# Layer 1 of a two-layer diffusion backbone: the output projection finishes one token tile at a time, and the MLP's first three blocks follow in pieces of 128 tokens

## The chip, the cores and the metric

The kernel runs on one core of a Trainium2 chip. The metric is the device time of one execution, in microseconds; before, the median of three runs is 1603.42 us (1602.07 to 1603.76).

## The reference

Two layers with the same weights for 256 context and 256 latent tokens, 1024 wide. Each layer mixes tokens with three parallel branches, merges them with gates, applies one output projection `W_out`, and then runs a squared-ReLU MLP. Around both halves stand RMS norms and shift, scale and gate vectors. The last layer (layer 1) needs only the latent tokens. The part that matters here, shortened:

```python
merged = g[..., 0, :] * (ys[0] @ w_branch[0])
for j in range(1, N_BRANCHES):
    merged = merged + g[..., j, :] * (ys[j] @ w_branch[j])
y_l = merged @ w_out
...
x = x + m_l[2] * rms_norm(y_l, norm_g[l, 1])
h_l = modulate(rms_norm(x, norm_g[l, 2]), m_l[3], m_l[4])
x = x + m_l[5] * rms_norm(jnp.square(jax.nn.relu(h_l @ w_mlp_up[l])) @ w_mlp_down[l], norm_g[l, 3])
```

So the MLP of a token needs the norm of the whole row of `y_l`, that is both halves of its output projection.

## The kernel before

All 512 tokens lie in four tiles of 128: tiles 0 and 1 are context, 2 and 3 are latent. Layer 1 works on tiles 2 and 3. Activations are kept as a high and a low part (`hact`, in the tile `h`), weights too, and each product is made of three matmuls: high by high, high by low, low by high. `mm_cm` (L248 to L250) holds weights in the array and streams tokens; `mm_tm` (L260 to L262) holds 128 tokens and streams 512 weight columns.

A weight block of 4096 numbers per partition arrives as two DMAs (L217, on SP's queue) into two of five slots `raw`; ScalarE casts each into the high part (L226), VectorE subtracts for the low part (L227). Blocks go in turn to the two places of `whl`, or to a place in the arena `arr` if `dst` is given. Every free place is only reused after its last reader.

In layer 1, `branch` (L1163 to L1190) makes the merged activations, eight channel tiles one after another: the sigmoid of the gate (L1163, ScalarE), the product with the branch's projection (L1180, VectorE, reading PSUM), the sum (L1185, GpSimd), high (L1189) and low part (L1190). L1128 and L1129 write the activations of the third branch that its projection reads. PSUM banks go round by `dps`.

`tm_out` with `W_out` follows: two halves of 512 output columns, each from two blocks of 512 rows. In layer 1 `seqs` asks for half 0 of tiles 2 and 3 and then half 1, where the last half is done tile by tile. One tile and half is 24 matmuls. `finish` takes each result: the sum of squares (L654, ScalarE) and the product with the gate row (L655, VectorE). `after(tt)` then runs the chain from the projection to the MLP's input for one tile: `post` (L630, L455 on GpSimd, L634), `prenorm` (squares L567, L569, L455, scaling L574 on VectorE and L576 on ScalarE, eight transposes L582 on TensorE) and `modulate` (L599 on VectorE and L597 on ScalarE from PSUM, high part L604, low part L606). In layer 1 the tiles' modulations are held back in `late` and done together when tile 3 is through.

The MLP's up projection runs through `cm_blocks`: 16 blocks of 256 columns, each two groups (`i`) of 24 matmuls. In layer 1 all of them stream the 256 latent tokens at once. `relu2` takes each group: L1330 and L1331 on ScalarE, L1332 on GpSimd, L1333 on VectorE. `nb` is 2: the first two blocks lie in `arr`, the later ones in `whl`. `gate_rows` (L620, eight transposes) makes the gate row that the MLP's end needs.

The order of the instructions on each engine is set by a scheduler from the dependencies, from priorities (`hp`) and from a few rules of order (`behind`, `set_fence`); each engine then works its own list strictly in that order.

Of the kernel before, what the change touches and what calls it, by code (L numbers as in the profile page):

```python
# [19 lines left out]
T = 512  # L20
LAT = 256
# [90 lines left out]
class Net:  # L112
# [524 lines left out]
    def tm_out(self, w, r0, act, y, yss, seqs, add, gains=None, after=None):  # L637


        nc = self.nc  # L640
        junk = self.A.get(1)
        left = {tt: 2 for tt in y}

        def finish(tt, b, ps):
            o = y[tt][:, b * 512:b * 512 + 512]
            with self.hp():
                src = ps
                if add:
                    nc.vector.tensor_tensor(out=o, in0=src, in1=o, op=ALU.add)
                    src = o  # L650
                elif not gains:
                    nc.scalar.copy(o, src)
                if gains:
                    nc.scalar.activation(junk[:, :], src, AF.Square, scale=D ** -0.5, accum_out=yss[tt][:, b:b + 1])  # L654
                    nc.vector.tensor_tensor(out=o, in0=src, in1=gains(tt)[:, b * 512:b * 512 + 512], op=ALU.mult)  # L655
            left[tt] -= 1

        for tts, halves, whole in seqs:
            for b in halves:
                ps = {}  # L660
                order = [(kh, tt) for kh in range(2) for tt in tts]
                blks = {}
                if whole:
                    order = [(kh, tt) for tt in tts for kh in range(2)]
                    blks = {kh: self.wblock(w, r0 + kh * 512, 4, b * 512, 512) for kh in range(2)}
                for kh, tt in order:
                    if kh not in blks:
                        blks[kh] = self.wblock(w, r0 + kh * 512, 4, b * 512, 512)
                    if not kh:
                        ps[tt] = self.dps()  # L670
                    self.mm_tm(ps[tt], blks[kh], 4, 0, 512, act, tt, kt0=kh * 4, start=not kh, stop=kh == 1)
                    if kh:
                        finish(tt, b, ps[tt])
            for tt in tts:
                if gains and left[tt] == 0:
                    after(tt)
        junk.free()
# [516 lines left out]
    def cm_blocks(self, loads, q0, skew, evac, done=lambda b: None, also=None):  # L1194


        segs = [(q0, T - q0)]
        b0 = 0
        if skew and q0 == 0:
            blks = [loads[b]() for b in range(2)]  # L1200
            for t0 in (0, LAT):
                for b, blk in enumerate(blks):
                    for i in range(2):
                        ps = self.dps()[:, 0:LAT]
                        self.mm_cm(ps, blk, 8, i * 128, self.hact, t0, LAT)
                        evac(b, i, ps, t0, LAT)
                    if t0:
                        done(b)
                if also:
                    also(range(t0 // 128, t0 // 128 + 2))  # L1210
            b0 = 2
        for b in range(b0, len(loads)):
            blk = loads[b]()
            for i in range(2):
                ps = self.dps()[:, 0:T - q0]
                self.mm_cm(ps, blk, 8, i * 128, self.hact, q0, T - q0)
                evac(b, i, ps, q0, T - q0)
            done(b)
# [22 lines left out]
    def layer(self, l):  # L1241
        nc, A, I = self.nc, self.A, self.I
        last = l == DEPTH - 1
        self.nd = 3 if last else 2
        w = I["w_in"][l]
        tts = list(range(4)) if not last else [2, 3]

        ysb_b, ys_b = self.acts(4)
        for hp in range(2):
            st, hv, gn, bufs = self.hgrn_dense(l, w, hp)  # L1250
# [10 lines left out]
        for hp in range(2):  # L1261
            Q, Kt, dv, bufs = pair
# [5 lines left out]
        Q, kT, sv = self.swa_dense(l, w)  # L1268
# [17 lines left out]
        sv = self.scale_vecs(l, 1)  # L1286
        y = {tt: A.get(2) for tt in tts}
        if not last:
            seqs = [((0, 1), (0, 1), False), ((2, 3), (0, 1), False)]
        else:  # L1290
            seqs = [((2, 3), (0,), False), ((2, 3), (1,), True)]
        yss = {tt: self.yss[:, tt * 3:tt * 3 + 3] for tt in tts}

        late = []

        def after(tt):
            with self.hp():
                ops = list(self.post(tt, y[tt], yss[tt]))
                if not last:
                    self.modulate(tt, sv, self.prenorm(tt, y[tt]), y[tt])  # L1300
                    return
                late.append((tt, sv, self.prenorm(tt, y[tt]), y[tt]))
                if tt == 3:
                    res = self.modulate(*late[0], ops=ops) + self.modulate(*late[1], quick=True)
                    self.set_fence(res, 1, 2)

        if not last:
            while self.pumps:
# [1 line left out]
            self.ada_late(1, range(3))  # L1310
            self.rate = 0
        self.nd, self.np = 4, 8
        nb = 2 if last else 1
        gains = lambda tt: G[1 if tt < 2 else 0]
        self.tm_out(I["w_out"][l], 0, self.hact, y, yss, seqs, False, gains, after)
        for g in G.values():
            g.free()

        q0 = 0 if not last else LAT
        n = T - q0  # L1320
        y = {tt: A.get(2) for tt in tts}
# [28 lines left out]
        for qd in range(4):  # L1350
            ab, act, wb = {}, {}, {}

            def wu(b):
                if not last and qd in (0, 3):
                    self.rate = 2 if (qd, b) >= (0, 2) else 0
                if qd == 0 and b < nb:
                    wb[b] = self.R.get(8)
                return self.wblock(I["w_mlp_up"][l], 0, 8, qd * 1024 + b * 256, 256, dst=wb[b].ap if b in wb else None)

            def done(b):  # L1360
                if b in wb:
                    wb[b].free()

            self.cm_blocks([lambda b=b: wu(b) for b in range(4)], q0, qd == 0,
                           lambda b, i, ps, t0, nn: relu2(ab, act, b * 2 + i, ps, t0, nn), done)
            if qd == 3:
                G = {s: self.gate_rows(l, 1, s) for s in ((1, 0) if not last else (0,))}
                if not last:
                    sv = self.scale_vecs(l + 1, 0)
            if last and qd == 3:  # L1370
                seqs = [((2, 3), (0,), False), ((2, 3), (1,), True)]
            elif qd == 3:
                seqs = [((0, 1), (0, 1), False), ((2, 3), (0, 1), False)]
            else:
                seqs = [(tts, (0, 1), False)]
            self.tm_out(I["w_mlp_down"][l], qd * 1024, act, y, yss, seqs, qd > 0, gains if qd == 3 else None, after)
            for b in ab.values():
                b.free()
# [37 lines left out]
```

## Time and profile before

| | |
|---|---|
| runs | 1602.07, 1603.42, 1603.76 us |
| profiled execution, own time | 1602.47 us |
| its span, first to last instruction | 1600.7 us |
| TensorE matmul busy | 1546.6 us (97%) |
| VectorE, ScalarE, GpSimd busy | 1045.6, 777.4, 393.0 us |
| mean granted TensorE clock | 0.986 of full speed |

A busy share is an average over the whole program, so the stage that is changed, about 1370 to 1430 us, is read by itself: how long TensorE waits there, what ends the waits, and how far apart its matmuls start. In the timeline a row gives start, length, engine, line, operation, tiles and shapes; a matmul's length contains a fixed part that overlaps the next, so its price in a stream is the distance from start to start. A 128x256 matmul is one that streams 256 columns.

### The profile page before, as it was taken

What the parts mean: (1) busy time and instruction counts of PE and PEld (TensorE: products, weight loads), DVE (VectorE), ACT (ScalarE), POOL (GpSimd) and SP (SyncE); (2) the same over time, 40 slices, a digit from 0 to 9 for tenths busy, and PEclk for the clock granted to TensorE, in tenths of its full rate; (3) what the DMA queues carried; (4) which work ended last, traced back from release to release, by engine and by line L of the source; (5) the groups of instructions that cost most, each with busy time, mean ns of one, the idle gap of its engine ahead of it and who ended that gap; (6) DMA issues with size and microseconds to landing.
All of it is one profiled execution on the core that took longest, in us unless ns stands there. A gap on an engine that the chain in (4) does not pass through costs nothing.

```text
span 1600.7 us, 26956 instructions
## 1 busy us (share of the span) xinstructions
PE 1546.6 (97%) x10326; PEld 1323.4 (83%) x10326; DVE 1045.6 (65%) x1897; ACT 777.4 (49%) x1588; POOL 393.0 (25%) x419
## 2 busy tenths in 40 slices
PE   6999999999999999999999999999898999989997
PEld 4788887878777778888888888999897999889996
DVE  3655544577477568777656546786668788665665
ACT  4443433446444457533424246644445656666553
POOL 1142415050420001210102011464455250121001
PEclk9999999999999999999999999999999999999999
DMA  9823234233332336466566434432334254446562
GB/s 282 236 80 119 75 114 143 80 79 115 123 93 79 115 109 211 140 202 194 176 208 191 151 106 145 125 114 78 122 106 106 67 149 125 148 139 191 185 185 92
DMA packets 209681, 220.06 MB, mean 137 GB/s; under 512 B 24400, under 2 KB 177168, under 8 KB 209552
## 3 DMA queue, kind: packets, MB, share of 16 engines
q1 hardware_dynamic: 209552, 218.34, 45.2%
q8 instruction: 81, 1.33, 0.3%
q14 instruction: 48, 0.39, 0.1%
HBM read 217.26 MB, written 1.05 MB: 136 GB/s over the span
## 4 chain that ended last, share of the span: by engine, by line
PE 85%; DVE 5%; POOL 4%; DMA 2%; ACT 2%; issue 2%; SPq 1%; POOLq 0%; DVEq 0%; ACTq 0%
PE b L248 16%; PE b L249 16%; PE b L250 16%; PE b L260 8%; PE b L261 8%; PE b L262 8%; POOL arf L919 1%; PE b L364 1%; DVE whl L227 1%; PE b L1122 1%; PE b L1109 1%; PE b L869 1%; PE b L949 1%; PE b L950 1%; PE b L853 1%
## 5 line engine op out<-in xcount | busy, mean ns | idle before, releaser
L227 DVE TENSOR_TENSOR whl<-raw,whl 128x512 fp32r<-128x512 f32 x588 | 431.4, 753 | 243.3 <-ACT whl L226 233.7
L226 ACT CAST whl<-raw 128x512 fp32r<-128x512 f32 x588 | 356.3, 620 | 256.4 <-PE b L262 129.3
L248 PE MATMUL b<-h,whl 128*128 128x512 f32 (+1 forms) x1296 | 447.6, 347 | 1.2 <-ACT arf L964 0.6
L250 PE MATMUL b<-h,whl 128*128 128x512 f32 (+1 forms) x1296 | 444.9, 344 | 0.8 <-DVE whl L227 0.8
L249 PE MATMUL b<-h,whl 128*128 128x512 f32 (+1 forms) x1296 | 444.6, 343 | 0.4 <-POOL h L606 0.3
L248 PEld LDWEIGHTS b<-h,whl 128*128 128x128 f32 x1296 | 247.9, 192 | 33.8 <-ACT whl L226 2.9
L250 PEld LDWEIGHTS b<-h,whl 128*128 128x128 f32 x1296 | 246.8, 191 | 29.5 <-issue 1.6
L249 PEld LDWEIGHTS b<-h,whl 128*128 128x128 f32 x1296 | 246.9, 191 | 28.9 <-issue 2.4
L1332 POOL TENSOR_TENSOR arf<-arf 128x256 f32<-128x256 f32 (+1 forms) x68 | 59.8, 880 | 411.3 <-ACT arr L1331 399.5
L262 PE MATMUL b<-whl,arr 128*128 128x512 f32 x384 | 149.9, 390 | 0.0
L261 PE MATMUL b<-whl,arr 128*128 128x512 f32 x384 | 149.9, 390 | 0.0
L260 PE MATMUL b<-whl,arr 128*128 128x512 f32 x384 | 149.7, 391 | 0.0
L919 POOL TENSOR_TENSOR arf<-arf,cst 32x256 f32<-32x256 f32 x104 | 94.3, 907 | 192.3 <-ACT arf L964 70.7
L260 PE MATMUL b<-whl,h 128*128 128x256 f32 (+1 forms) x416 | 129.0, 313 | 0.0
L261 PE MATMUL b<-whl,h 128*128 128x256 f32 (+1 forms) x416 | 128.7, 311 | 0.0
L262 PE MATMUL b<-whl,h 128*128 128x256 f32 (+1 forms) x416 | 128.6, 311 | 0.0
L455 POOL TENSOR_TENSOR sm<-sm,nhalf 128x1 f32<-128x1 f32 (+2 forms) x42 | 37.0, 883 | 333.5 <-DVE sm L630 242.5
L809 POOL TENSOR_TENSOR arf<-arf 128x512 f32<-128x512 f32 x56 | 75.8, 1376 | 43.7 <-ACT arf L788 24.1
L260 PEld LDWEIGHTS b<-whl,h 128*128 128x128 f32 x416 | 80.0, 192 | 6.4 <-ACT arf L753 0.8
L260 PEld LDWEIGHTS b<-whl,arr 128*128 128x128 f32 x384 | 72.1, 188 | 15.9 <-issue 1.2
L262 PEld LDWEIGHTS b<-whl,arr 128*128 128x128 f32 x384 | 72.1, 188 | 14.9
L261 PEld LDWEIGHTS b<-whl,arr 128*128 128x128 f32 x384 | 72.1, 188 | 14.5
(224 smaller groups left out, 2434.1 us busy)
## 6 DMA issues: line engine op xcount, KB each, us to landing
raw<-in_w_in_dram SPq DMA_DIRECT2D x110, 512.0 KB, 3.9
arf<-in_w_ada_dram SPq DMA_DIRECT2D x80, 512.0 KB, 4.9
raw<-in_w_mlp_down_dram SPq DMA_DIRECT2D x72, 512.0 KB, 3.8
raw<-in_w_mlp_up_dram SPq DMA_DIRECT2D x64, 512.0 KB, 4.3
raw<-in_w_out_dram SPq DMA_DIRECT2D x24, 512.0 KB, 4.2
arf<-in_w_ada_dram SPq DMA_DIRECT2D x32, 256.0 KB, 5.6
raw<-in_w_branch_dram SPq DMA_DIRECT2D x16, 512.0 KB, 3.9
raw<-in_w_in_dram SPq DMA_DIRECT2D x32, 128.0 KB, 3.3
```

Source lines behind the costliest of these rows:

```text
L226: self.behind(ops, lambda: nc.scalar.copy(r32(h), src))
L227: self.split_op = self.behind(ops, lambda: nc.vector.tensor_tensor(out=r32(l), in0=src, in1=h, op=ALU.subtract))
L248: nc.tensor.matmul(ps, wh, xh[:, t0:t0 + n], start=start and k == 0, stop=False)
L249: nc.tensor.matmul(ps, wh, xl[:, t0:t0 + n], start=False, stop=False)
L250: nc.tensor.matmul(ps, wl, xh[:, t0:t0 + n], start=False, stop=stop and k == nk - 1)
L260: nc.tensor.matmul(ps, xh, wh, start=start and k == 0, stop=False)
L261: nc.tensor.matmul(ps, xh, wl, start=False, stop=False)
L262: nc.tensor.matmul(ps, xl, wh, start=False, stop=stop and k == nk - 1)
L455: self.nc.gpsimd.tensor_tensor(out=r, in0=ms, in1=self.nhalf[:, 0:cols], op=ALU.pow)
L809: nc.gpsimd.tensor_tensor(out=kx, in0=kx, in1=view(cur, 1, [(nb - 1, 2), (2, nb // 2), (0, h)]), op=ALU.mult)
L919: nc.gpsimd.tensor_tensor(out=b[o, 0:LAT], in0=x[i], in1=self.cst[i, C_RS:C_RS + LAT], op=ALU.mult)
L1332: nc.gpsimd.tensor_tensor(out=r[:, c], in0=r[:, c], in1=r[:, c], op=ALU.mult)
```

## The change

In layer 1 the output projection now does tile 2 completely, both halves, and then tile 3. All four blocks of `W_out` are therefore held at once: the two of half 0 in `whl`, the two of half 1 in `arr`. `after` runs the whole chain for each tile when that tile is through. In `cm_blocks` the first three blocks of layer 1's MLP take the 128 tokens of tile 2, then the 128 of tile 3; the fourth block and all later ones take 256 as before. `nb` becomes 1: only the first block lies in `arr`, the second and third in `whl`.

```diff
@@ tm_out
         for tts, halves, whole in seqs:
+            if whole == "all":
+                bufs = [self.R.get(8) for _ in range(2)]
+                blks = {(b, kh): self.wblock(w, r0 + kh * 512, 4, b * 512, 512, dst=bufs[kh].ap if b else None)
+                        for b in halves for kh in range(2)}
+                for tt in tts:
+                    for b in halves:
+                        ps = self.dps()
+                        for kh in range(2):
+                            self.mm_tm(ps, blks[b, kh], 4, 0, 512, act, tt, kt0=kh * 4, start=not kh, stop=kh == 1)
+                        finish(tt, b, ps)
+                    after(tt)
+                for b in bufs:
+                    b.free()
+                continue
@@ cm_blocks
-        segs = [(q0, T - q0)]
         b0 = 0
-        if skew and q0 == 0:
-            blks = [loads[b]() for b in range(2)]
-            for t0 in (0, LAT):
+        if skew:
+            b0, step = (2, LAT) if q0 == 0 else (3, 128)
+            blks = [loads[b]() for b in range(b0)]
+            for t0 in range(q0, T, step):
                 for b, blk in enumerate(blks):
                     for i in range(2):
-                        ps = self.dps()[:, 0:LAT]
-                        self.mm_cm(ps, blk, 8, i * 128, self.hact, t0, LAT)
-                        evac(b, i, ps, t0, LAT)
-                    if t0:
+                        ps = self.dps()[:, 0:step]
+                        self.mm_cm(ps, blk, 8, i * 128, self.hact, t0, step)
+                        evac(b, i, ps, t0, step)
+                    if t0 + step == T:
                         done(b)
...
-            b0 = 2
@@ layer
-            seqs = [((2, 3), (0,), False), ((2, 3), (1,), True)]
+            seqs = [((2, 3), (0, 1), "all")]
...
-        late = []
-
         def after(tt):
             with self.hp():
-                ops = list(self.post(tt, y[tt], yss[tt]))
-                if not last:
-                    self.modulate(tt, sv, self.prenorm(tt, y[tt]), y[tt])
-                    return
-                late.append((tt, sv, self.prenorm(tt, y[tt]), y[tt]))
-                if tt == 3:
-                    res = self.modulate(*late[0], ops=ops) + self.modulate(*late[1], quick=True)
-                    self.set_fence(res, 1, 2)
+                for _ in self.post(tt, y[tt], yss[tt]):
+                    pass
+                res = self.modulate(tt, sv, self.prenorm(tt, y[tt]), y[tt], quick=last)
+                if last and tt == 3:
+                    self.set_fence(res, 3, 2)
...
-        nb = 2 if last else 1
+        nb = 1
```

TensorE, from the last matmul of the output projection into the MLP, layer 1 (`cst` by `arf` are the transposes of the chain, `cst` by `sm` those of the gate row, `h` the activations). Before:

```order
L262 MATMUL b_86<-whl,h 128x512
L582 MATMUL b_89<-cst,arf 128x128 x4
L582 MATMUL b_90<-cst,arf 128x128 x4
L582 MATMUL b_91<-cst,arf 128x128 x4
L582 MATMUL b_88<-cst,arf 128x128 x4
L620 MATMUL b_89<-cst,sm 128x128 x4
L620 MATMUL b_90<-cst,sm 128x128 x4
L248 MATMUL b_87<-h,arr 128x256
L248 MATMUL b_84<-h,arr 128x256
L249 MATMUL b_87<-h,arr 128x256
```

After:

```order
L262 MATMUL b_86<-arr,h 128x512
L582 MATMUL b_89<-cst,arf 128x128 x4
L582 MATMUL b_90<-cst,arf 128x128 x4
L620 MATMUL b_89<-cst,sm 128x128 x4
L620 MATMUL b_90<-cst,sm 128x128 x4
L248 MATMUL b_87<-h,arr 128x128
L248 MATMUL b_84<-h,arr 128x128
L248 MATMUL b_85<-h,whl 128x128
L248 MATMUL b_86<-h,whl 128x128
L249 MATMUL b_87<-h,arr 128x128
```

Only tile 2's transposes are left between the projection and the MLP, tile 3's follow 30 matmuls into the MLP. Tile 2's transposes still stand behind all of tile 3's projection. The gate row's transposes still use the two banks that the modulation has to read first.

ScalarE, between the third branch's activations (L1128) and its gates (L1163), layer 1. In the new file these lines are 14 higher: L1142 is L1128 and L1177 is L1163. Before:

```order
L621 COPY arf<-b_87 128x512
L621 COPY arf<-b_88 128x512
L1128 CAST arr<-b_91 128x128 x2
L1163 ACT_TABLE_LOAD
L1163 ACTIVATE arf<-arf 128x256 x8
```

After:

```order
L621 COPY arf<-b_87 128x512
L621 COPY arf<-b_88 128x512
L1142 CAST arr<-b_91 128x128
L226 CAST arr<-raw 128x512 x2
L1142 CAST arr<-b_91 128x128
L1177 ACT_TABLE_LOAD
L1177 ACTIVATE arf<-arf 128x256 x8
```

Two casts of the first block of `W_out` for `arr` now stand ahead of the last L1128; before, the block that arrives in the same slot was cast later.

VectorE, the end of the chain from the scaling (L574) to the low part (L606), layer 1. Before, for both tiles:

```order
L574 TENSOR_SCALAR arf<-arf,sm 128x512 x2
L599 TENSOR_SCALAR arf<-b_89,sb,M_67 128x128 x3
L599 TENSOR_SCALAR arf<-b_90,sb,M_67 128x128 x3
L599 TENSOR_SCALAR arf<-b_91,sb,M_67 128x128 x4
L604 CAST h<-arf 128x4x128
L606 TENSOR_TENSOR h<-arf,h 128x4x128 x3
```

After, for tile 2:

```order
L574 TENSOR_SCALAR arf<-arf,sm 128x512
L227 TENSOR_TENSOR arr<-raw,arr 128x512 x2
L599 TENSOR_SCALAR arf<-b_89,sb,M_67 128x128 x4
L630 TENSOR_REDUCE sm<-yss 128x1
L655 TENSOR_TENSOR arf<-b_86,arf 128x512
L227 TENSOR_TENSOR whl<-raw,whl 128x512
L604 CAST h<-arf 128x4x128
L227 TENSOR_TENSOR whl<-raw,whl 128x512
L634 SCALAR_TENSOR_TENSOR arf<-arf,sm 128x512 x2
L606 TENSOR_TENSOR h<-arf,h 128x4x128 x2
```

ScalarE after, over the same stretch:

```order
L576 ACTIVATE arf<-arf,sm 128x512
L654 ACTIVATE arf,yss<-b_86 128x512
L226 CAST whl<-raw 128x512 x2
L597 ACTIVATE arf<-b_90,M_67,sb 128x128 x4
L604 CAST h<-arf 128x4x128
L567 ACTIVATE arf,sm<-arf 128x512 x2
```

Between tile 2's modulation (L599) and its low part (L606) VectorE now does two weight subtractions and three steps of tile 3's chain (L655 and L634 twice); ahead of tile 2's L597 ScalarE now does two weight casts.

## Rows read from the trace of the kernel before

**Rows 1.** The page: busy time by engine, share of the span, instructions.

```profile
PE 1546.6 (97%) x10326; PEld 1323.4 (83%) x10326; DVE 1045.6 (65%) x1897; ACT 777.4 (49%) x1588; POOL 393.0 (25%) x419
```

**Rows 2.** Windows: length, busy by engine with counts, PEclk (granted clock), DMA share, GB/s.

```profile
1402.30:1413.50 11.20, 5.50 (x28) 4.96 (x28) 9.66 (x24) 8.59 (x21) 3.09 (x4) 0.70 0.14 53
1404.42:1411.25 6.83, 3.84 (x18) 3.84 (x19) 5.36 (x16) 4.48 (x12) 1.71 (x4) 0.50 0.16 62
1413.51:1430.42 16.91, 16.91 (x143) 16.91 (x143) 9.99 (x19) 11.24 (x24) 3.29 (x5) 1.00 0.47 156
```

**Rows 3.** TensorE's timeline from the projection's end into the MLP.

```profile
1402.04 0.39 PE L262 MATMUL b<-whl,h 128*128 128x512 f32 x1
1407.41 3.68 PE L582 MATMUL b<-cst,arf 128*128 128x128 f32 x16 [4.98 <-DVE arf L574]
1412.50 0.50 PE L248 MATMUL b<-h,arr 128*128 128x256 f32 x2 [0.40 <-DVE h L604]
1413.32 0.36 PE L249 MATMUL b<-h,arr 128*128 128x256 f32 x1 [0.32 <-DVE h L606]
```

**Rows 4.** TensorE's timeline around one L1087, the only form streaming 128 split columns.

```profile
1318.26 0.22 PE L1087 MATMUL b<-half 128*128 128x128 f32 x1
1318.32 0.33 PE L248 MATMUL b<-arr,whl 128*128 128x256 f32 x1
1318.49 0.28 PE L249 MATMUL b<-arr,whl 128*128 128x256 f32 x1
```

**Rows 5.** The weight loads (PEld) of the same stretch.

```profile
1318.27 0.19 PEld L248 LDWEIGHTS b<-arr,whl 128*128 128x128 f32 x1
1318.37 0.19 PEld L249 LDWEIGHTS b<-arr,whl 128*128 128x128 f32 x1
```

**Rows 6.** ScalarE's and TensorE's timelines before the projection.

```profile
1370.20 0.27 ACT L1128 CAST arr<-b 128x128 fp32r<-128x128 f32 x1 [0.36 <-DVE arr L1129]
1370.48 1.28 ACT L1163 ACT_TABLE_LOAD   x1
1371.77 2.57 ACT L1163 ACTIVATE arf<-arf 128x256 f32<-128x256 f32 x8
...
1373.19 0.39 PE L248 MATMUL b<-arr,whl 128*128 128x256 f32 x1
```

**Rows 7.** SP's timeline: the issue into the slot concerned; DMA issues: KB, us to landing.

```profile
1367.17 0.37 SPq L217 DMA_DIRECT2D raw<-in_w_out_dram  x1
...
raw<-in_w_mlp_up_dram SPq DMA_DIRECT2D x64, 512.0 KB, 4.3
raw<-in_w_out_dram SPq DMA_DIRECT2D x24, 512.0 KB, 4.2
```

**Rows 8.** VectorE's and ScalarE's timelines: the chain's pieces.

```profile
1372.71 1.09 DVE L1180 TENSOR_TENSOR arf<-b,arf 128x256 f32<-128x256 f32 x3 [1.92 <-PE b L250]
1395.39 0.68 DVE L655 TENSOR_TENSOR arf<-b,arf 128x512 f32<-128x512 f32 x1
1404.55 1.42 DVE L634 SCALAR_TENSOR_TENSOR arf<-arf,sm 128x512 f32<-128x512 f32 x2
1408.57 3.28 DVE L599 TENSOR_SCALAR arf<-b,sb,M 128x128 f32<-128x128 f32 x10 [0.29 <-PE b L582]
1411.88 0.56 DVE L604 CAST h<-arf 128x512 fp32r<-128x512 f32 x1
1412.48 2.04 DVE L606 TENSOR_TENSOR h<-arf,h 128x512 fp32r<-128x512 f32 x3
1410.73 1.55 ACT L597 ACTIVATE arf<-b,M,sb 128x128 f32<-128x128 f32 x4
1415.79 2.18 ACT L226 CAST whl<-raw 128x512 fp32r<-128x512 f32 x4
1424.86 0.38 ACT L1330 ACTIVATE arf<-b 128x256 f32<-128x256 f32 x1 [1.81 <-PE b L250]
1425.27 0.42 ACT L1331 ACTIVATE arr<-arf 128x256 fp32r<-128x256 f32 x1
```

## Prediction

> **What bounds the kernel now.** I read the page first: TensorE has a matmul in flight for 97% of the span, the next engine for 65% [rows 1]. So nearly everything that TensorE does is on the path, and the change can win only what TensorE waits in its stage, and loses whatever it adds to TensorE's list.
>
> Next TensorE's timeline around the hand-over from projection to MLP. The projection's last matmul starts at 1402.04; then nothing until the transposes at 1407.41, which waited for VectorE's scaling, and the MLP streams steadily only from 1413.32, when the low part (L606) is there [rows 3]. That is 11.3 us, in which TensorE does 24 transposes and two matmuls. This is all there is to win: TensorE is busy for 5.5 us of the 11.2 us window by its in-flight time, and part of the stretch runs at half the clock: 0.50 of full speed from 1404.42 to 1411.25, after the engine had stood idle since about 1402.4 [rows 2]. From 1413.51 on the clock is 1.00 and there are no gaps: the 16.91 us to 1430.42 hold 143 matmul records, two of which began earlier, so 256-column matmuls start 16.91/141 = 0.12 us apart [rows 2]. At 1430.42 the fourth block begins. From 1402.04 to there it is **28.4 us now**; the change rewrites exactly this piece.
>
> **The price of a 128-column matmul.** Three blocks are two groups of 24 matmuls each, 144 in all, of 256 columns. They become 288 of 128 columns: the same columns, twice the matmuls, and every matmul brings its own weight load (as many loads as matmuls, [rows 1]). So the question is whether a load of 128 columns hides behind a matmul of 128. The trace has one place with split operands and 128 columns, L1087. Read from start to start it costs 0.06 us (1318.26 to 1318.32), half of 0.12, which would be ideal. But the matmul behind it then needs 0.17 us to the next one (1318.32 to 1318.49) where 0.12 is usual [rows 4]: 0.05 us come back one place later, so L1087 costs 0.11. The weight loads say why: the load behind L1087 starts as L1087 starts (1318.27), the next one 0.10 us later [rows 5]. A 128-column matmul is over before the next weights are in. In a run of such matmuls each waits for a load, and I take 0.108 us for each, between the 0.10 and the 0.11. Bounds: 0.06, if loads hide after all, and 0.12, what a 256-column matmul takes. I take neither end because the two readings of rows 4 and 5 agree.
>
> The Trainium skill differs: "TensorE: Matmul & The Clock Gate", section "Back-to-back issue gap", gives about 81 ns for each matmul of 128 columns in a sustained stream of load and matmul pairs. By that figure the sum below would be +4.5 us instead of +12.2; no run of this case shows such a stream yet, and the rows above are nearer to this kernel.
>
> **The change part by part.**
>
> *The projection's order.* Same 96 matmuls, same blocks; only when they are cast changes. The first block for `arr` arrives in a slot that SP refills from 1367.17, landing 4.2 us later, at 1371.4 [rows 7]. Its two casts now stand ahead of ScalarE's last L1128, which ran at 1370.20 [rows 6]. Each cast is 2.18/4 = 0.545 us [rows 8], so ScalarE is through at 1372.5, with L1128 at 1372.7, the table load of 1.28 us at 1374.0, the first gate of about 0.4 at 1374.4, and VectorE's product L1180 of 0.4 [rows 6, 8] at 1374.9. The matmul at 1373.19 [rows 6] needs the bank that this frees, and starts at 1374.9: **+1.7 us**, with nothing behind it to hide in, since TensorE has no slack until the end of the projection. Bounds: 0, if the block lands before 1370, to 2.5, if the whole delay of L1128 counts. Two MLP loads move ahead of the last three `W_out` loads on SP's queue; each waits for a slot that comes free before the one behind it, so I price that at nothing; cover is the same slots' own wait.
>
> *The hand-over.* E' is the start of the projection's last matmul after the change (1402.04 + 1.7). Tile 2's projection ends 39 matmuls earlier, so squares, row factor and scaling of tile 2 are done by E' and its eight transposes follow at once. What is late next is the rest of its chain, because the lists now mix it with other work:
> - VectorE: L599 four times, 0.33 each [rows 8], from E'+0.95 to 2.25; tile 3's L655, 0.68, to 2.9; then a subtraction of weights that needs a cast by ScalarE.
> - ScalarE: that cast needs the second half of MLP block 2. Its slot is given up by the `arr` subtractions at about E'-1.5 (estimate: the casts follow tile 2's squares), plus 4.3 us to land [rows 7] = E'+2.8. Two casts to 3.9, four L597 (1.55) to 5.45 [rows 8].
> - VectorE again: subtraction to 4.05, L604 (0.56) to 4.6, second subtraction to 5.3, tile 3's two L634 (1.42) to 6.7, and only then tile 2's low part L606 (0.68) to about 7.3 [rows 8].
>
> The gate row's transposes wait for L597 too, and stay hidden before 7.3. So TensorE streams from **E'+7.3** (now: 11.3 after E). Four high-part matmuls slip in before. Bounds: 3.5, if nothing stands between (2.25 + 0.56 + 0.68), and 8.
>
> *The MLP's blocks.* 284 matmuls at 0.108 are 30.7 us. Tile 3's eight transposes lie among them, 0.9 us; its chain has the 26 matmuls ahead of them and the 114 behind them to hide in. Together **E'+38.9** for the start of the fourth block.
>
> *Evacuation.* Twice as many, half as wide. ScalarE needs 0.38 + 0.42 us for a 256-column group [rows 8] against 24 x 0.108 = 2.6 us of matmuls: priced at nothing; if the matmuls went at 0.06 it would still fit (1.4 us).
>
> *The clock.* The wait remains, so the clock may fall again. In the window of 6.83 us at 0.50 [rows 2] matmuls could take double: 0 to +3.4 us. I take 0: now, too, the clock was back within the stall.
>
> **The sum.** 38.9 - 28.4 = +10.5, plus 1.7 = **+12.2 us**. Everything later is TensorE-bound and unchanged, so it passes through. The profiled execution's own time is 1602.47 us, so 1614.7 us; the median of the runs lies 0.95 us above that execution, so 1615.6 us.
>
> **Rivals.**
>
> *Loads hide (not slower).* A 128-column matmul costs 0.06 us, as rows 4 read from start to start. The blocks then take 17.0 us instead of 30.7: +12.2 - 13.6 = -1.4 us, 1602.0 us. It decides from about 0.065 us per matmul downward; below 0.054, or if tile 2's chain comes through as early as E'+3.5, it is faster (to 1598). For it: the start after L1087. Against it: the 0.05 us that come back, and loads 0.10 apart.
>
> *Loads half hidden.* Loads overlap better in a long run than behind a single L1087, say 0.084 us, the middle of 0.06 and 0.108: 284 x 0.084 = 23.9, which makes +5.4 us, 1608.8 us. Nothing in rows 5 shows a load under 0.10. The 81 ns of the Trainium skill's page on TensorE (same section) would be this case.
>
> *The clock stays low.* With half its time spent waiting for loads, TensorE might be granted 0.50 through the whole stretch. If loads then take double too, up to 30 us are added: 1619 to 1646 us. For it: the fall at 1404.42. Against it: that fall followed an engine at rest, not a slow one.
>
> *The change doesn't do what it says.* In the order of the instructions tile 2's transposes still stand behind all of tile 3's projection, and its low part behind tile 3's L634. That is half this rival, and it is in the sum already.
>
> **How the numbers follow.** The forecast has 0.74; its own range, from the bounds of stall (-3.8), price (+3.4) and early wait (-1.7 to +0.8), is about 1611 to 1620 us. Half hidden: 0.10. Loads hide: 0.11. Low clock: 0.05. The range of 1607.5 to 1620.5 us holds the forecast and the half-hidden case. A measurement of this kernel tells about 0.2%, 3.2 us, from no change. Forecast, half hidden and low clock are slower by more than that: 0.88, less 0.02 for a forecast at all its low bounds. Loads hide gives 0.05 faster and 0.06 same.
>
> **What would show it.** In the changed profile: L248 to L250 with 128 columns start 0.10 to 0.115 us apart (right), or 0.06 (wrong, and then the time is near 1602). The wait between the last L262 and the steady stream is about 7 us, ended by L606. ScalarE waits for a `W_out` load just ahead of the sigmoid's table load, and the projection ends near 1403.7. The piece from the projection's last matmul to the fourth block is near 39 us. The granted clock is 1.00 while the 128-column matmuls run. If that piece is under 30 us, or the projection ends no later, the forecast is wrong.

## The result and the profile after

The changed kernel takes 1647.94 us (median of five runs, 1645.97 to 1650.76), beside 1603.42 us for the kernel before (five runs, 1602.07 to 1604.96): a ratio of 1.0279, 95% interval 1.0267 to 1.0290. That is 44.5 us slower. The forecast was 12.2 us slower and a range up to 1620.5 us, so the sign came out as forecast and the size did not. The line numbers of the new file are the same up to L658, 14 higher in `branch` (L1142 is L1128, L1177 is L1163) and 8 higher in `relu2`.

The page of the changed kernel, its first part's first line and the granted clock in 40 slices:

```profile
PE 1590.1 (97%) x10470; PEld 1365.9 (83%) x10470; DVE 1047.0 (64%) x1903; ACT 778.7 (47%) x1601; POOL 392.8 (24%) x424
...
PEclk9999999999999999999999999999999999659999
```

TensorE's busy time went up from 1546.6 us [rows 1] to 1590.1 us at the same share of 97%, and VectorE's and ScalarE's hardly moved. 144 more matmuls are in the list, as forecast. The busy time alone could mean more work; the clock line shows that it is slower work, in two slices after the hand-over.

The windows of the same kernel (columns as in rows 2): the stretch at the low clock, the 128-column stream in it, and what follows.

```profile
1409.18:1477.45 68.27, 66.82 (x314) 66.82 (x315) 16.32 (x36) 17.56 (x47) 5.66 (x13) 0.50 0.11 32
1412.30:1474.56 62.26, 62.26 (x293) 62.26 (x294) 12.12 (x28) 13.36 (x37) 5.25 (x12) 0.50 0.08 24
1477.45:1600.00 122.55, 122.55 (x766) 111.26 (x766) 69.88 (x115) 71.11 (x134) 11.88 (x19) 1.00 0.59 185
```

Before, the clock was 0.50 for 6.83 us, all inside the wait [rows 2]. Now it is 0.50 (1.2 GHz) for 68.27 us, and the whole 128-column stream lies in it, although TensorE has a matmul in flight in all of the 62.26 us.

TensorE's timeline of the changed kernel, from the projection's last matmul to the rise of the clock:

```profile
1404.03 0.39 PE L262 MATMUL b<-arr,h 128*128 128x512 f32 x1
1404.26 1.03 PE L582 MATMUL b<-cst,arf 128*128 128x128 f32 x8
1406.32 0.65 PE L620 MATMUL b<-cst,sm 128*128 128x128 f32 x4 [1.02 <-DVE sm L630]
1410.63 1.12 PE L620 MATMUL b<-cst,sm 128*128 128x128 f32 x4 [3.66 <-ACT arf L597]
1411.40 0.67 PE L248 MATMUL b<-h,arr 128*128 128x128 f32 x2
...
1412.30 0.47 PE L249 MATMUL b<-h,arr 128*128 128x128 f32 x1
1412.57 0.42 PE L250 MATMUL b<-h,arr 128*128 128x128 f32 x1
1412.78 0.41 PE L248 MATMUL b<-h,arr 128*128 128x128 f32 x1
...
1474.13 0.41 PE L249 MATMUL b<-h,whl 128*128 128x128 f32 x1
1474.35 0.41 PE L250 MATMUL b<-h,whl 128*128 128x128 f32 x1
1474.56 0.52 PE L248 MATMUL b<-h,whl 128*128 128x256 f32 x1
...
1477.44 0.29 PE L249 MATMUL b<-h,whl 128*128 128x256 f32 x1
1477.57 0.28 PE L250 MATMUL b<-h,whl 128*128 128x256 f32 x1
```

Three things are to be seen. The wait did get shorter: the steady stream begins 8.27 us after the projection's last matmul (1404.03 to 1412.30), 11.28 us before [rows 3]. The 128-column matmuls start 0.21 us apart, from the first to the last (1412.57 to 1412.78, 1474.13 to 1474.35). And the clock is back 2.9 us after the first of the 256-column matmuls that follow (1474.56 to 1477.45).

The weight loads of the same stretch:

```profile
1412.67 0.33 PEld L248 LDWEIGHTS b<-h,arr 128*128 128x128 f32 x1
1412.89 0.33 PEld L249 LDWEIGHTS b<-h,arr 128*128 128x128 f32 x1
```

Loads were 0.10 us apart behind L1087 at 1.00 [rows 5]; here they are 0.22 apart at 0.50. So the spacing of the loads goes by the granted clock as well.

**Where the 45.4 us of the two spans lie** (1646.1 less 1600.7). The stage begins 0.9 us later; its start (the last L1087 product) differs by up to 3.9 us among the profiled executions, so this is not put down to the change. From there to its last matmul the projection takes 1.1 us longer (51.40 against 50.31). The wait gives 3.0 us back. The stream from there to the fourth block takes 62.26 us instead of 17.10 (1413.32 to 1430.42, [rows 2, 3]): 45.2 us more. And the fourth block's first matmuls, still at 0.50, cost 1.3 us.

### The profile page after: what moved, and what is told of

The parts are those of the page before. It is cut to its first block, busy times and chain, and to the rows that moved or that the text cites. A ratio compares the mean times of both kernels' runs of the same rounds, so it can differ in the third digit from the quotient of the medians.

```text
span 1646.1 us, 27282 instructions
## 1 busy us (share of the span) xinstructions
PE 1590.1 (97%) x10470; PEld 1365.9 (83%) x10470; DVE 1047.0 (64%) x1903; ACT 778.7 (47%) x1601; POOL 392.8 (24%) x424
## 4 chain that ended last, share of the span: by engine, by line
PE 85%; POOL 4%; DVE 4%; DMA 3%; ACT 2%; issue 2%; POOLq 0%; DVEq 0%; ACTq 0%; SPq 0%
PE b L248 16%; PE b L249 16%; PE b L250 16%; PE b L260 8%; PE b L261 8%; PE b L262 8%; POOL arf L933 2%; DMA arf<-in_w_ada_dram 1%; POOL arf L823 1%; PE b L364 1%; PE b L1136 1%; PE b L1123 1%; DVE whl L227 1%; PE b L883 1%; PE b L963 1%
## 5 line engine op out<-in xcount | busy, mean ns | idle before, releaser
L227 DVE TENSOR_TENSOR whl<-raw,whl 128x512 fp32r<-128x512 f32 x584 | 426.1, 749 | 256.4 <-ACT whl L226 247.0
L248 PE MATMUL b<-h,whl 128*128 128x512 f32 (+2 forms) x1344 | 469.7, 351 | 1.2 <-ACT arf L978 0.6
L250 PE MATMUL b<-h,whl 128*128 128x512 f32 (+2 forms) x1344 | 466.3, 347 | 0.9 <-DVE whl L227 0.8
L249 PE MATMUL b<-h,whl 128*128 128x512 f32 (+2 forms) x1344 | 466.1, 347 | 0.4 <-POOL h L606 0.3
L248 PEld LDWEIGHTS b<-h,whl 128*128 128x128 f32 x1344 | 266.3, 199 | 33.6 <-ACT whl L226 2.9
L249 PEld LDWEIGHTS b<-h,whl 128*128 128x128 f32 x1344 | 265.5, 198 | 29.0 <-issue 2.6
L250 PEld LDWEIGHTS b<-h,whl 128*128 128x128 f32 x1344 | 265.1, 197 | 29.4 <-issue 1.6
L1340 POOL TENSOR_TENSOR arf<-arf 128x256 f32<-128x256 f32 (+2 forms) x74 | 62.1, 840 | 451.7 <-ACT arr L1339 446.0
L260 PE MATMUL b<-whl,h 128*128 128x256 f32 (+1 forms) x400 | 123.2, 310 | 0.0
L262 PE MATMUL b<-whl,h 128*128 128x256 f32 (+1 forms) x400 | 122.6, 308 | 0.0
L261 PE MATMUL b<-whl,h 128*128 128x256 f32 (+1 forms) x400 | 122.5, 308 | 0.0
L1338 ACT ACTIVATE arf<-b 128x256 f32<-128x256 f32 (+2 forms) x74 | 32.9, 445 | 128.1 <-PE b L250 128.1
```

The costliest lines, as they stand in the source:

```text
L227: self.split_op = self.behind(ops, lambda: nc.vector.tensor_tensor(out=r32(l), in0=src, in1=h, op=ALU.subtract))
L248: nc.tensor.matmul(ps, wh, xh[:, t0:t0 + n], start=start and k == 0, stop=False)
L249: nc.tensor.matmul(ps, wh, xl[:, t0:t0 + n], start=False, stop=False)
L250: nc.tensor.matmul(ps, wl, xh[:, t0:t0 + n], start=False, stop=stop and k == nk - 1)
L260: nc.tensor.matmul(ps, xh, wh, start=start and k == 0, stop=False)
L261: nc.tensor.matmul(ps, xh, wl, start=False, stop=False)
```

## The experiments

Two questions: is the price of a 128-column matmul its weight load, and what holds the clock at 0.50? Fillers are 384-column matmuls on constants (`half`) whose results are overwritten; `issue_after` places them on TensorE's list behind the named instruction, `tr_op` being the last transpose of the tile and `mm_last` the projection's last matmul. Of each edit the lines that matter are shown; lines that only name an instruction are left out. Ratios are to runs of the kernel before on the same chip (medians 1602.7 to 1603.4 us). One execution of each kernel is profiled.

**Full clock into the stream.** The changed kernel with the wait filled.

```diff
+                if last and tt == 2:
+                    for _ in range(36):
+                        with self.tc.issue_after(self.tr_op.ins):
+                            nc.tensor.matmul(self.ps[0][:, 0:384], r32(self.half[:, 0:128]), r32(self.half[:, 0:384]), start=True, stop=True)
```

> The change, plus 36 matmuls of 384 columns on constants, right behind tile 2's transposes, so that TensorE works through the wait (36 x about 0.17 = 6.2 us of the 8.3 us); their results are overwritten. Theory 'entry': the clock stayed at 0.50 only because the wait let it fall and a stream of 128-column matmuls cannot lift it; entered at 1.00 it stays there. Then the 288 matmuls start 0.107 us apart, the clock is 1.00 through the stretch, and the time is 1603 + 12 to 16 = 1615 to 1619 us. Theory 'stream': the 128-column stream takes the clock down by itself; the clock falls within the stretch and the time stays above 1632 us.

Measured: 1617.31 us (1616.34 to 1617.49), ratio 1.0082, interval 1.0065 to 1.0099. Its windows, the wait and then the 128-column stream, and its timeline (L1315 is the filler):

```profile
1403.80:1412.72 8.92, 8.60 (x57) 8.39 (x57) 7.81 (x17) 5.83 (x15) 0.76 (x2) 1.00 0.57 181
1412.72:1445.29 32.57, 32.57 (x295) 32.57 (x294) 10.28 (x25) 13.06 (x35) 5.02 (x12) 1.00 0.10 33
```

```profile
1405.12 6.50 PE L1315 MATMUL b<-half 128*128 128x384 f32 x36
...
1412.84 0.28 PE L250 MATMUL b<-h,arr 128*128 128x128 f32 x1
1412.95 0.27 PE L248 MATMUL b<-h,arr 128*128 128x128 f32 x1
1413.06 0.28 PE L249 MATMUL b<-h,arr 128*128 128x128 f32 x1
```

The same MLP matmuls in the same order, with 36 more ahead of them: the clock is 1.00 in the wait and stays there through the stream, the matmuls start 0.11 us apart, and 30.6 us of the 44.5 are gone. So about 70% of the loss is the clock, and a stream that enters at 1.00 keeps it here. What remains is 13.9 us above the kernel before, near the forecast.

**One half of the change at a time.** First the projection's order and the chain as changed, with every MLP block at 256 columns; then the reverse.

```diff
-        self.cm_blocks([lambda b=b: wu(b) for b in range(4)], q0, qd == 0,
+        self.cm_blocks([lambda b=b: wu(b) for b in range(4)], q0, qd == 0 and not last,
```

> The change's projection order and chain, but the MLP's blocks stream 256 tokens as before. Both clock theories: without 128-column matmuls a low clock lasts one or two windows of a wait (about 7 us) as before, and the time is 1600 to 1610 us: +1.1 us from the early wait on ScalarE, and a stall between 9 and 14 us instead of 11.3. Rival 'projection order': if the held blocks and the new waits make the loss, the time stays above 1630 us.

Measured: 1608.49 us (1606.38 to 1610.61), ratio 1.0032, interval 1.0022 to 1.0041. Its TensorE timeline, and the window of its low clock:

```profile
1405.37 0.39 PE L262 MATMUL b<-arr,h 128*128 128x512 f32 x1
...
1415.74 1.97 PE L582 MATMUL b<-cst,arf 128*128 128x128 f32 x8 [2.43 <-DVE arf L574]
1418.78 0.80 PE L248 MATMUL b<-h,arr 128*128 128x256 f32 x2 [1.07 <-DVE h L604]
...
1419.80 0.41 PE L249 MATMUL b<-h,arr 128*128 128x256 f32 x1
```

```profile
1410.57:1424.23 13.66, 8.54 (x37) 7.74 (x38) 7.63 (x16) 6.27 (x16) 0.55 (x1) 0.50 0.13 38
```

Here both tiles must be through before the stream starts, and the wait grows to 14.4 us (11.28 before): tile 3's scaling L574 now stands on VectorE behind tile 2's modulation and the weight subtractions. The new order by itself costs 5 us; only with the pieces does it shorten the wait. The low clock enters the stream here too, but this stream has 256 columns, and the clock is back at 1424.23, 4.4 us after the steady stream began.

The reverse is the kernel before with its projection and chain, the first three blocks in 128-token pieces, and `nb` 1.

```diff
@@ cm_blocks, layer 1
+            b0, step = (2, LAT) if q0 == 0 else (3, 128)
...
-        nb = 2 if last else 1
+        nb = 1
```

> The projection order and chain of before, and only the MLP's first three blocks in pieces of 128 tokens. If the clock is low when the stream begins and cannot rise: 288 x 0.213 - 144 x 0.12 = +44 us, 1647 us, with 0.50 through the whole stretch. If the clock is back at 1.00 before the stream begins, as it was before the change (1411.25, the stream at 1412.5), theory 'entry' says it stays, 288 x 0.107 - 17.3 = +13.6 us, 1617 us; theory 'stream' says that it falls again and the time is above 1635 us.

Measured: 1616.41 us (1615.83 to 1619.74), ratio 1.0082, interval 1.0066 to 1.0098. Its windows, the low clock and then the stream to the fourth block:

```profile
1408.51:1415.33 6.82, 4.80 (x23) 4.80 (x24) 5.40 (x16) 5.23 (x13) 2.54 (x3) 0.50 0.00 0
1415.33:1447.59 32.26, 32.26 (x291) 32.26 (x290) 13.73 (x29) 15.69 (x41) 5.06 (x11) 1.00 0.29 98
```

Nothing was added to the wait here, and the clock falls as it did before. But it falls early enough to be back at 1415.33, just as the steady stream begins, and then 128-column matmuls run at 1.00 for 32.3 us. A low clock that ends with the wait did not slow the stream; what counts is where in time it lies. The second window answers the question of the price too: 291 matmul records in 32.26 us, 0.111 us each.

**One block instead of three** in pieces:

```diff
-            b0, step = (2, LAT) if q0 == 0 else (3, 128)
+            b0, step = (2, LAT) if q0 == 0 else (1, 128)
```

> The change with one block instead of three in pieces of 128 tokens. With the clock at 0.50 while they run: 96 x 0.213 instead of 48 x 0.12, +14.7 us, less what the shorter wait wins (11.3 to 8.3 us), plus 1.1 us of the early wait and up to 1.5 us until 256-column matmuls bring the clock back: 1616 to 1620 us, a third of the loss. If the loss were not in these matmuls it would stay near 1648 us.

Measured: 1618.85 us (1609.35 to 1622.10), ratio 1.0089, interval 1.0060 to 1.0117. Its TensorE timeline at the last 128-column matmuls, and the window of the low clock:

```profile
1432.72 0.41 PE L249 MATMUL b<-h,arr 128*128 128x128 f32 x1
1432.93 0.41 PE L250 MATMUL b<-h,arr 128*128 128x128 f32 x1
1433.14 0.52 PE L249 MATMUL b<-h,whl 128*128 128x256 f32 x1
```

```profile
1407.37:1438.09 30.72, 28.33 (x132) 28.14 (x133) 9.12 (x20) 8.84 (x25) 2.44 (x5) 0.50 0.07 24
```

The same picture, a third as long: all 96 of them 0.21 us apart at 0.50, and the clock rises only 5 us into the 256-column blocks. A third of the pieces gives back 29 of the 44.5 us. One of the five executions took only 1609.35 us, at a mean granted clock of 0.987 over the program where the other four had 0.976 to 0.981. It was not profiled, but 9.5 us less is about what 96 matmuls gain at 1.00 (96 x 0.10 us). This suggests that the same program can meet the fall or miss it; all five executions of the changed kernel met it (0.965 to 0.969).

**Wide matmuls in the middle of the slow stream.** 24 fillers behind tile 3's transposes, which lie early in the stream; the wait ahead of it is left as it is.

```diff
+                if last and tt == 3:
+                    for _ in range(24):
+                        with self.tc.issue_after(self.tr_op.ins):
+                            nc.tensor.matmul(self.ps[6][:, 0:384], r32(self.half[:, 0:128]), r32(self.half[:, 0:384]), start=True, stop=True)
```

> The change with its wait as it is (the clock falls), plus 24 matmuls of 384 columns on constants inside the stream, behind tile 3's transposes, some 30 matmuls into it. Theory 'entry': the stream begins at 0.50 (0.213 us apart), the wide matmuls (24 x about 0.3 us) lift the clock, and the other 258 then start 0.111 us apart at 1.00: 258 x 0.10 us less, about 7 us for the added ones, so 1626 to 1631 us. If a low clock came back by itself in the stream, the second part would be at 0.213 us again and the time near 1650 us. If matmuls of 128 columns could lift the clock, they would have done so in the change.

Measured: 1626.42 us (1624.03 to 1628.21), ratio 1.0149, interval 1.0132 to 1.0166. Its windows: the stream before the fillers, the fillers before and after the clock rises, the stream behind them.

```profile
1410.00:1416.80 6.80, 6.80 (x33) 6.80 (x34) 1.24 (x5) 0.73 (x1) 0.55 (x1) 0.50 0.11 41
1416.91:1420.25 3.34, 3.34 (x12) 3.34 (x11) 2.71 (x6) 2.13 (x5) 0.00 (x0) 0.50 0.00 0
1420.25:1422.88 2.63, 2.63 (x17) 2.63 (x17) 0.00 (x0) 0.00 (x0) 0.00 (x0) 1.00 0.00 0
1422.88:1451.47 28.59, 28.59 (x258) 28.59 (x258) 6.60 (x17) 10.54 (x29) 4.41 (x11) 1.00 0.12 38
```

The stream enters at 0.50, the clock rises during the wide matmuls (at 1420.25), and the 128-column matmuls behind them run at 1.00 to their end. 6 us of useless work save 21.5 us. Together with the first run this shows that the same stream holds whichever of the two levels it enters with, in these runs.

**The early wait, and the chain.** The first run again, with the casts of the `W_out` blocks for `arr` held behind the gates' sigmoids (`sig_op` is the last of these):

```diff
+        if last:
+            self.set_fence([self.sig_op], 2, 2)
         self.tm_out(I["w_out"][l], 0, self.hact, y, yss, seqs, False, gains, after)
```

> The kernel that fills the wait with 36 matmuls, and the two W_out blocks for the arena are cast only behind the gates' sigmoids. If the early wait on ScalarE costs what it seems, the time from the last L1087 to the last projection matmul goes from 51.4 back to 50.3 us, and the total from 1617.3 to about 1616.2 us; if those 1.1 us come from the projection's new order of matmuls, the distance stays at 51.4.

Measured: 1623.16 us (1620.95 to 1624.20), ratio 1.0123, interval 1.0108 to 1.0138: a miss. Its TensorE timeline:

```profile
1401.06 0.39 PE L262 MATMUL b<-arr,h 128*128 128x512 f32 x1
1406.25 0.66 PE L582 MATMUL b<-cst,arf 128*128 128x128 f32 x4 [4.80 <-ACT arf L576]
1406.66 4.59 PE L1315 MATMUL b<-half 128*128 128x384 f32 x16
1411.09 0.60 PE L582 MATMUL b<-cst,arf 128*128 128x128 f32 x4
```

The early wait is gone: last L1087 to last projection matmul 50.34 us, as before the change, so those casts were its cause. But with the casts moved, tile 2's transposes came 5.2 us after the projection instead of 0.7, and 16 fillers slid in between the two halves of them; the steady stream started 15.2 us after the projection. Part of the miss is thus the experiment's own filler.

The next run has 16 fillers, and the casts of MLP block 2 stand behind tile 2's modulation instead of ahead of its L597:

```diff
-                    for _ in range(36):
+                    for _ in range(16):
...
+                if last and tt == 2:
+                    self.mod2 = res
                 if last and tt == 3:
-                    self.set_fence(res, 3, 2)
+                    self.set_fence(self.mod2, 2, 1)
```

> As the kernel before it in this call, with 16 filling matmuls instead of 36, and MLP block 2 cast behind tile 2's modulation, so that L597 no longer stands behind a weight load. If that load and tile 3's steps make the wait, the steady stream begins 4 to 5 us after the projection's last matmul instead of 8.3 (clock 1.00), and the time is 1611 to 1613.5 us. If the wait is the chain's own length, it stays near 8 us and 1616 us; then the clock may fall again.

Measured: 1615.84 us (1614.34 to 1617.38), ratio 1.0079, interval 1.0064 to 1.0095. The early wait stays away (50.33 us), the steady stream begins 9.0 us after the projection, hardly sooner than in the first run (9.2): what the reordered casts won, tile 2's transposes lost by coming 2.5 us after the projection. Also a miss on size. The clock is 0.50 only in this window, in which mostly fillers run, and the stream is at 1.00:

```profile
1406.82:1410.23 3.41, 3.41 (x14) 3.41 (x13) 2.99 (x8) 3.33 (x8) 0.55 (x1) 0.50 0.61 181
```

**Fewer loads for the same product.** Is the price of the pieces the load? The high part of the weights streams the high and the low part of 128 tokens at once (256 columns), only the low part streams 128: 16 loads for a group instead of 24, and 384 columns as before. The two halves are added when the group is taken. The rest is as in the run before.

```diff
+                            ps = self.dps()[:, 0:256]
+                            hi, lo = blk
+                            for k in range(8):
+                                both = r32(view(self.h, k * T + t0, [(8 * T, 2), (1, 128)]))
+                                self.nc.tensor.matmul(ps, hi[:, k, i * 128:i * 128 + 128], both, start=k == 0, stop=False)
+                                self.nc.tensor.matmul(ps[:, 0:128], lo[:, k, i * 128:i * 128 + 128],
+                                                      self.hact[k][0][:, t0:t0 + 128], start=False, stop=k == 7)
```

> As the kernel before it in this call, but each high weight tile is loaded once and streams high and low part of the 128 tokens together (256 columns), then the low weight streams 128 columns: 192 loads instead of 288 for the three blocks; the two halves of the bank are added by one ScalarE copy and one VectorE sum for each group. If the price is set by the loads: 96 x (0.12 + 0.111) = 22.2 us instead of 32.0, 1601 to 1604 us, about the kernel before. If the columns set it, it is no faster than the kernel with 288 matmuls.

Measured: 1606.81 us (1604.56 to 1609.72), ratio 1.0023, interval 1.0014 to 1.0032. Its window of the stream, and the matmuls and the weight loads in it (L1223 is the 256-column matmul, L1224 the other):

```profile
1411.19:1434.33 23.14, 23.14 (x202) 23.14 (x201) 14.37 (x38) 14.17 (x43) 4.48 (x10) 1.00 0.22 67
```

```profile
1411.42 0.23 PE L1224 MATMUL b<-h,arr 128*128 128x128 f32 x1
1411.48 0.34 PE L1223 MATMUL b<-h,arr 128*128 128x256 f32 x1
1411.65 0.22 PE L1224 MATMUL b<-h,arr 128*128 128x128 f32 x1
...
1411.42 0.19 PEld L1223 LDWEIGHTS b<-h,arr 128*128 128x128 f32 x1
1411.53 0.19 PEld L1224 LDWEIGHTS b<-h,arr 128*128 128x128 f32 x1
1411.65 0.19 PEld L1223 LDWEIGHTS b<-h,arr 128*128 128x128 f32 x1
```

9.0 us less than the run before, for the same columns and a third of the loads less: 23.1 us for the pieces instead of about 33. The price does not go by the columns. Loads and matmuls fell by the same third, so the total alone does not say which of the two sets it; the rows do. The matmul behind a 128-column one starts 0.06 us after it (1411.42 to 1411.48), so a matmul as such does not take 0.11 us, while the loads start 0.11 to 0.12 us apart. It ends 3 us above what was hoped for, and above the kernel before: 96 pairs at 0.231 us are still 4.9 us more than 144 matmuls at 0.12, tile 3's transposes in the stream add 0.9, and the wait won only 2.7 us (8.57 against 11.28).

**Two last attempts to beat the kernel before.** That kernel with 32 fillers in its idle time, and the last version with two blocks in pieces and no filler:

```diff
+                if tt == 3:
+                    for _ in range(32):
+                        with self.tc.issue_after(self.mm_last.ins):
+                            nc.tensor.matmul(self.ps[0][:, 0:384], r32(self.half[:, 0:128]), r32(self.half[:, 0:384]), start=True, stop=True)
```

> The kernel before with 32 matmuls of 384 columns on constants between the projection's last matmul and the transposes (their result is overwritten): they fill the 5.4 us in which TensorE stood idle, so the granted clock should stay at 1.00 through the hand-over, where it was 0.50 for 6.83 us. What does the half clock cost the kernel before? Theory: almost nothing, since VectorE's ten L599 (3.28 us) and the low parts set the end of that stretch; only the first four transposes stand ahead of them, about 0.4 us: 1602.4 us, ratio 0.9975 to 1.000. Rival: everything in the 6.83 us goes at half speed and half of it comes back: minus 3.4 us, 1599.5 us, ratio 0.998; then filling the wait alone would beat both kernels.

Measured: 1606.03 us (1602.74 to 1607.86), beside 1602.98 us for the kernel before (21 runs), ratio 1.0016, interval 1.0006 to 1.0026. Its windows: the old place of the low clock, and the new one.

```profile
1404.42:1411.25 6.83, 6.45 (x44) 6.17 (x43) 5.46 (x15) 4.62 (x12) 1.83 (x3) 1.00 0.23 77
1415.65:1419.06 3.41, 3.41 (x19) 3.41 (x18) 3.41 (x6) 2.90 (x6) 0.00 (x0) 0.50 0.14 37
```

(The two ratios in the expectation overlap; its times are what sets the theories apart.) Neither theory had this: in the profiled execution, filling the idle time did not remove the low clock but moved it, out of the wait and into the 256-column stream (at 1415.65, with the stream running since 1415.07). There it costs time, and the steady stream also starts 0.7 us later than before (12.0 us after the projection). In the kernel before, the low clock lies where it is almost free: VectorE's L599 starts 6.5 us after the projection's last matmul there (1408.57, [rows 8]), and 6.4 us after it here, with the clock at 1.00 in the wait.

> The version with the high weights streaming 256 columns (high and low part of 128 tokens at once), without any filler and with two blocks in pieces instead of three. From that version's 1606.8 us: one block less in pieces gives back 1.65 us (64 matmuls at 0.116 us against 48 at 0.12), the 16 fillers 0.6 us: 1604.6 us, if every second matmul of 256 columns is enough to lift the clock soon after the stream begins. If the stream stays at 0.50 as the changed kernel's did, the 128 matmuls cost 0.1 us more each: about 1617 us. To beat the kernel before it would have to be under 1600 us, which neither theory gives.

Measured: 1606.95 us (1604.23 to 1613.02), ratio 1.0028, interval 1.0017 to 1.0039.

```profile
1411.59:1415.00 3.41, 3.41 (x18) 3.41 (x17) 2.13 (x6) 1.05 (x3) 0.55 (x1) 0.50 0.65 178
```

That window of its trace shows the low clock in the stream again: without fillers the clock falls about a microsecond into the stream, a pair takes 0.43 us instead of 0.23, and after 3.41 us it is back. So this stream, half of it 256 columns wide, does lift the clock, where the changed kernel's did not. The 1.6 us that the third block should give back are about what 18 matmuls lose there (18 x 0.1 us). The executions spread over 9 us and only this one is profiled, so whether the low clock is as short in the others is not shown. No version beat the kernel before.

## Why the prediction failed on the size

*The price of a 128-column matmul: right.* Taken at 0.108 us; at full clock it is 0.111 (32.57 us for 284 matmuls and eight transposes in the first run). Both rivals with hidden or half hidden loads are out for this kernel. So are the 81 ns that the Trainium skill, "TensorE: Matmul & The Clock Gate", section "Back-to-back issue gap", gives for such a stream: 0.111 us at the upper clock, 0.213 at the lower. That the price is the load is shown by the version with a third fewer of them, together with the starts of its loads.

*The early wait: right in mechanism, a little too dear.* +1.7 was forecast, 51.40 less 50.31 is +1.1. ScalarE's timeline of the changed kernel:

```profile
1371.54 1.14 ACT L226 CAST arr<-raw 128x512 fp32r<-128x512 f32 x2 [0.79 <-DMA raw<-in_w_out_dram]
1372.58 0.26 ACT L1142 CAST arr<-b 128x128 fp32r<-128x128 f32 x1
1372.86 1.28 ACT L1177 ACT_TABLE_LOAD   x1
...
1408.03 1.14 ACT L226 CAST whl<-raw 128x512 fp32r<-128x512 f32 x2 [2.88 <-DMA raw<-in_w_mlp_up_dram]
```

The block's casts start at 1371.54 (forecast 1371.4), and L1142 and the table load end 0.1 us behind the forecast times (1372.84 and 1374.14). But in this trace the whole stage lies 0.9 us later than in the trace of before, from which the forecast counted, so less of that time is the wait. Casting later removed the wait.

*The hand-over: right, 1 us short.* 7.3 us forecast, 8.27 measured, ended by VectorE's L606 as said (it starts at 1411.56). The row at 1408.03 is the link that was mis-sized: MLP block 2 landed 4.0 us after the projection's last matmul, not 2.8.

*The clock: this step failed.* "In the window of 6.83 us at 0.50 [rows 2] matmuls could take double: 0 to +3.4 us. I take 0: now, too, the clock was back within the stall." Two things are wrong in it. The fall was assumed to keep its place; but the clock falls at 1409.18, 2.2 us ahead of the first MLP matmul, instead of 2.4 us into the wait at 1404.42. Tile 2's transposes now follow the projection at once (1404.26), so the idle stretch begins later, which fits: in all four profiled runs where those transposes follow at once and nothing fills the wait, the clock fell 4.3 to 5.2 us after the projection's last matmul, and in the two with the old order 2.4 and 2.9 us after it. Yet the lag behind TensorE's last work is not fixed (2.0 us before, 2.2 after, 1.1 with one block; in the run with the late casts TensorE idled for 4.8 us and the clock fell only 0.5 us after that), so these traces give no way to foretell the place. And its length was assumed to be that of the window before; but it lasted until 256-column matmuls had followed the 128-column stream.

The rival "the clock stays low" had the mechanism, the doubled loads and a price of up to 30 us, and was given a chance of 0.05 because the fall "followed an engine at rest, not a slow one". That is still true of the fall. What the argument missed is the return: in the trace of before the clock came back while transposes ran, and no row of it showed the split 128-column matmuls of the MLP in a stream, at either clock.

The Trainium skill, same page, section "Part 1: The HAM clock gate (the "warmup" mystery)", has the clock follow how busy TensorE was of late. If busy means a matmul in flight, the trace does not bear this out for this stream, which had one in flight in 62.26 of 62.26 us and stayed at 0.50.

*The sum, redone.* The clock's part is 62.26 less 32.57 us in the stream and 1.3 us behind it, 31.0 us. The other 14.4 us of the 45.4 are, to 0.1 us, the forecast's 12.2, +1.0 for the wait, +1.0 for price and transposes, -0.6 for the early wait and the 0.9 us that arose ahead of the stage. With the clock at 1.00 (and a wait of 9.2 us instead of 8.3) the change was measured at 1617.31 us, 1.7 us from the forecast. A slip without weight: the chances of the three slower cases add up to 0.89, not 0.88.

Why this stream, which waits for loads, holds the clock it enters with is not settled. That it does is shown at both levels (at 0.50 by the changed kernel and one block, at 1.00 by fillers in the wait, fillers in the stream, and the pieces without the new order). The width and the spacing alone do not explain it: before, the clock came back at 1411.25 behind 16 transposes that are 128 columns wide as well, each with its own load, and started 0.22 us apart (1407.41 to 1410.88). What in TensorE's work the chip goes by was not tried.

## What to carry to other kernels

When a change narrows matmuls, count the weight loads: 24 loads of 0.11 us stay 24 whether they stream 256 columns or 128. When it moves work into a wait of TensorE, look at which matmuls come behind the wait, and allow for the clock's fall landing in them: a fall that was free inside the wait can land in the stream, and the narrow stream here kept it to the end. A busy share of 100% does not show that a stretch runs at half the clock; read the granted clock beside it.

## What was not expected of the hardware

- A gapless stream of 128-column matmuls, each with its own load, stayed at a granted clock of 0.50 for 62.26 us, and the same stream stayed at 1.00 for 32.57 us when it entered there.
- At 0.50 a 256-column matmul and a 128-column one cost the same, 0.213 us from start to start; at 1.00 they cost 0.120 and 0.111. So a 128-column matmul with its load costs about what 256 columns do, at either level.
- With an idle wait filled with work the low clock began 11.2 us later (1404.42 to 1415.65) and lasted half as long (6.83 to 3.41 us), but it was still there (one profiled execution of each).
